# A hand-written order for the opening stage of a Fourier–Hyena and latent-attention block, and another order of its projections

## The chip, the cores and the metric

The kernel runs on one core of one Trainium2 chip. Its time is device microseconds (us) of one launch. A core has five engines with a queue each: TensorE (PE, matmuls and, beside them, weight loads, PEld), VectorE (DVE), ScalarE (ACT), GpSimd (POOL) and SyncE (SP, which here issues the DMAs). They run side by side and wait for each other by semaphores. SBUF is the on-chip memory with 128 partitions; PSUM is the smaller one into which PE accumulates.

## The reference

Two layers over an image sequence x (512 tokens of 1024) and a context (256 tokens of 1024). Layer 0 mixes tokens with a Fourier and a Hyena half, layer 1 with latent attention; each has a convolutional FFN. The change sits in layer 0's mixer. Cut to that:

```python
def _adaln(cond, w_mod, b_mod):
    return jnp.split((jax.nn.silu(cond) @ w_mod + b_mod)[:, None, :], 6, axis=-1)

def _hyena_filter_spectrum(L, w1, b1, w2, b2, w3, b3, w4, freq):
    ...                                        # z: 33 features of each position
    h = jnp.sin(f * (z @ _f32(w1) + _f32(b1)))
    h = jnp.sin(f * (h @ _f32(w2) + _f32(b2)))
    h = jnp.sin(f * (h @ _f32(w3) + _f32(b3)))
    h = h @ _f32(w4)
    h_fwd = h[:, :D_HYENA] * decay
    h_bwd = h[:, D_HYENA:] * decay
    two_sided = jnp.concatenate([h_fwd, zeros(1, D_HYENA), h_bwd[:0:-1]], axis=0)
    two_sided = two_sided / jnp.sum(jnp.abs(two_sided), axis=0, keepdims=True)
    return jnp.fft.rfft(two_sided, axis=0)

def _fourier_hyena_mixer(h, w_in, w_out, conv_w, conv_b, ...):
    proj = h @ w_in                                              # 1024 -> 2048
    y_f = fft2(proj[..., :512], axes=(1, 3)).real                # in 4 groups of 128
    x0, x1, v = jnp.split(_dwconv3(proj[..., 512:], conv_w, conv_b), 3, axis=-1)
    y_h = x0 * _long_conv(v * x1, spectrum, hy_bias)
    return jnp.concatenate([y_f, y_h], axis=-1) @ w_out

# layer 0, with shift, scale and gate of _adaln for x and for the context
hx = _rms_norm(x, norm1) * (1 + sc1) + sh1
x = x + g1 * _fourier_hyena_mixer(hx, ...)
x = x + g2 * _conv_ffn(...)
# the context goes the same way with its own modulation and a filter of its own length
```

## The kernel before

Activations lie transposed: eight tiles of 128 features, x in columns 0 to 511 and the context in 514 to 769 of the same tile (772 columns). To keep float32 accuracy, most operands are split in two, a rounded high part (`hi`, L98, on ACT) and the rest (`lo`, L103, on DVE), and a product is three matmuls (`mm3`: L117 high by high, L118 weights' high by low, L119 weights' low by high). In the tables of the profile a matmul shows as `mm<-hh,wh`: output, then input and weights. Two PSUM pools serve all: `mm` (1024 columns, 3 buffers) and `ms` (512 columns, 2 buffers). Streamed weights come through the pool `W` of three buffers each for the raw tile `wr` and its two halves `wh` and `wl` (`wload`, L105).

**The opening.** What must be there before the first projection: the normed and modulated inputs hh and hl, eight tiles each. What must be there before the spectral stage: the filters' spectra. Its parts:

- `filter_mlp` (L318): three layers, each one matmul (L331) and a sine, which is seven steps on DVE and the Sin on ACT (L306 to L316). It ends in h3, for 6 blocks of 128 positions (4 of x's filter, 2 of the context's).
- `filter_time` (L336), for each block: two 512-column matmuls with w4 (L346), one for the forward and one for the backward half; the products with the decay (L352, L353); in the first block the backward half's first row set to zero (L355); sum and difference of the halves on POOL (L358), each split (`aph`, `apl`, `amh`, `aml`); the absolute values of both halves (ACT, L365 and L366), their sum (POOL, L367), a matmul with a constant tile that sums over positions (L372), and a reciprocal S (L374).
- `filter_spec` (L377): the row of hy_bias, `brow`, is scaled (L382); the Nyquist row (L390 to L393); then for each of 2 or 4 frequency blocks a `wload` of the transform's table, the `mm3` over the filter's blocks, and the scaling by S (L404 to L406).
- `gemv_pe` (L171): one of four chunks of adaLN's shift and scale. Its 2 MB weights come in two DMAs (L177) into a pool `wm` of three, then eight matmuls (L180), a copy (L183), four small matmuls (L186) and the bias add (L191). `make_A` (L209) follows.
- `norm` (L212): `stat` squares a tile (ACT, L224) and sums it on PE (L225); `fin` copies, transposes the sums to columns (L233), runs an inverse square root of twelve tiny DVE steps (L121 to L138) and spreads it with a matmul against the identity (L239), R; `apply` for each of the eight tiles, x and context, scales by A and R (DVE, L249), adds the shift into hh (ACT, L251) and forms hl (DVE, L252).

They are called in this order: network; adaLN chunk 0; the context's filter in time; chunk 1; the context's spectrum; x's filter in time; chunk 2; x's statistics and R; chunk 3; the context's statistics and R; A; two frequency blocks of x's spectrum; sixteen `apply`; the other two. A scheduler of the kernel's framework lays out each engine's queue from that, so the order on an engine is not just the order of the calls.

**The projections.** `proj(m)` (L474), sixteen times: `wload` of a 1024 by 128 part of w_in, 48 matmuls over hh and hl, and a `gemv_dve` (L193), which computes one 128-feature tile of the rest of adaLN on DVE (a DMA into `wr`, L201, L202), so that DVE is used beside PE; 16 of the 32 such tiles `gl` go here, the rest into the `hook` of the w_out projection (two for each call). `hconv(m)` is a projection with its three-tap convolution (ACT L295, DVE L296 and L297). For each of four feature blocks v and x1 are projected, multiplied and folded (`fold`: POOL L490 and L491, DVE L495 and L496), and later transposed on PE (`turn`: six transposes L502) and split into `uTh` and `uTl`, which the spectral stage reads. The order of the calls:

```python
for i in range(4):
    hconv(12 + i, cv)
    if folded:
        turn(i - 1, folded.pop())
    hconv(8 + i, cx)
    folded.append(fold(i, cv, cx))
hconv(4, x0[0])
turn(3, folded.pop())
for i in range(1, 4):
    hconv(4 + i, x0[i])
for g in range(4):
    nc.scalar.copy(Uf[g], proj(g)[:, :TW])
```

**After that.** `spectral` for the context and for x, the inverse transforms, `fourier` for four groups (Uf), the w_out projection, FFN 0 (w_up, L710 on; a `fill` does three `gemv_dve` tiles of layer 1 with each of the first blocks), attention and FFN 1.

## Time and profile before

| | |
|---|---|
| time, median of 3 runs | 1839.36 us (1838.71 to 1841.66) |
| the profiled execution: its own time | 1836.58 us |
| its span (first to last instruction) | 1834.8 us |
| mean granted clock of PE over the span | 0.957 |
| busy in the span: PE, PEld, DVE, ACT, POOL | 93%, 72%, 55%, 33%, 7% |
| chain that ended last: PE, DVE, ACT, POOL | 78%, 11%, 4%, 3% |
| read from HBM, mean rate | 167.23 MB, 93 GB/s |
| opening / projections / rest of the mixer (from, to) | 0 to 135 / 135 to 275 / 275 to 386 us |
| w_out and FFN 0 / attention / o-projection and FFN 1, roughly | 386 to 1000 / 1000 to 1420 / 1420 to 1834 us |

A line of a timeline gives the start, the duration of one instruction, its engine, its line in the kernel (L331 is line 331), its operation, the tiles as output<-inputs, and its shape; a bracket names the idle time of the engine before it and what ended that. PE's granted clock is the share of its full speed that it was allowed in a stretch. PE at 93% means that some 120 us of the span are without a matmul; the table of windows in the prediction shows that 37 of them lie in the opening.

### The profile page before, as it was taken

What the parts mean: (1) busy time and instruction counts of PE and PEld (TensorE: products, weight loads), DVE (VectorE), ACT (ScalarE), POOL (GpSimd) and SP (SyncE); (2) the same over time, 40 slices, a digit from 0 to 9 for tenths busy, and PEclk for the clock granted to TensorE, in tenths of its full rate; (3) what the DMA queues carried; (4) which work ended last, traced back from release to release, by engine and by line L of the source; (5) the groups of instructions that cost most, each with busy time, mean ns of one, the idle gap of its engine ahead of it and who ended that gap; (6) DMA issues with size and microseconds to landing.
All of it is one profiled execution on the core that took longest, in us unless ns stands there. A gap on an engine that the chain in (4) does not pass through costs nothing.

```text
span 1834.8 us, 21694 instructions
## 1 busy us (share of the span) xinstructions
PE 1714.6 (93%) x8742; PEld 1328.5 (72%) x8742; DVE 1015.0 (55%) x1663; ACT 613.2 (33%) x830; POOL 122.7 (7%) x202
## 2 busy tenths in 40 slices
PE   5789996799899999999999887899998999999999
PEld 2358885687688888888888565555554778888887
DVE  4668735887886434543233554666664554444443
ACT  2332212322422212221122334665663443223231
POOL 1401103310000000000000000110110000000000
PEclk8889996799999999999999998899999999999999
DMA  9213320355255223432112320000002323322322
GB/s 355 75 58 127 114 84 20 118 179 166 104 172 170 106 92 134 153 104 69 47 63 78 110 74 24 1 12 12 12 12 69 115 69 99 108 92 92 104 75 98
DMA packets 53249, 172.83 MB, mean 94 GB/s; under 512 B 6043, under 2 KB 8925, under 8 KB 52125
## 3 DMA queue, kind: packets, MB, share of 16 engines
q1 hardware_dynamic: 53149, 171.45, 27.2%
q8 instruction: 69, 1.13, 0.2%
q14 instruction: 31, 0.25, 0.0%
HBM read 167.23 MB, written 4.19 MB: 93 GB/s over the span
## 4 chain that ended last, share of the span: by engine, by line
PE 78%; DVE 11%; ACT 4%; POOL 3%; issue 2%; DMA 1%; SPq 0%; POOLq 0%; ACTq 0%; DVEq 0%
PE mm L117 22%; PE mm L118 21%; PE mm L119 21%; PE pv L1053 2%; PE z L1041 2%; PE ms L225 2%; DVE wl L103 1%; DVE S L1031 1%; DVE junk L201 1%; PE s L1007 1%; DVE hl L252 1%; ACT S L1022 1%; PE s L117 1%; PE s L118 1%; PE s L119 1%
## 5 line engine op out<-in xcount | busy, mean ns | idle before, releaser
L117 PE MATMUL mm<-hh,wh 128*128 128x512 f32 (+2 forms) x1344 | 473.5, 355 | 4.4 <-ACT hh L251 4.1
L118 PE MATMUL mm<-hl,wh 128*128 128x512 f32 (+2 forms) x1344 | 473.2, 353 | 2.6 <-DVE hl L252 2.3
L119 PE MATMUL mm<-hh,wl 128*128 128x512 f32 (+2 forms) x1344 | 472.8, 352 | 1.3 <-DVE wl L103 1.3
L98 ACT ACTIVATE wh<-wr 128x1024 fp32r<-128x1024 f32 (+2 forms) x200 | 206.3, 1032 | 714.2 <-PE mm L118 657.2
L103 DVE TENSOR_TENSOR wl<-wr,wh 128x1024 fp32r<-128x1024 f32 (+2 forms) x200 | 242.3, 1212 | 308.4 <-ACT wh L98 300.7
L117 PEld LDWEIGHTS mm<-hh,wh 128*128 128x128 f32 x1344 | 253.9, 189 | 53.2 <-issue 11.1
L118 PEld LDWEIGHTS mm<-hl,wh 128*128 128x128 f32 x1344 | 254.1, 189 | 41.2 <-DVE hl L252 5.0
L119 PEld LDWEIGHTS mm<-hh,wl 128*128 128x128 f32 x1344 | 253.8, 189 | 38.1 <-issue 2.5
L117 PE MATMUL mm<-ah,wh 128*128 128x512 f32 (+1 forms) x528 | 187.9, 356 | 0.0
L118 PE MATMUL mm<-al,wh 128*128 128x512 f32 (+1 forms) x528 | 187.8, 356 | 0.0
L119 PE MATMUL mm<-ah,wl 128*128 128x512 f32 (+1 forms) x528 | 187.4, 355 | 0.0
L201 DVE SCALAR_TENSOR_TENSOR junk<-wr,sb 128x1024 bf16<-128x1024 f32 x128 | 157.6, 1231 | 30.4 <-DMA wr<-wmodT 30.0
L685 DVE SCALAR_TENSOR_TENSOR xr<-mm,mod,xr 128x512 f32<-128x512 f32 (+1 forms) x100 | 62.1, 641 | 198.9 <-PE mm L119 198.7
L117 PEld LDWEIGHTS mm<-ah,wh 128*128 128x128 f32 x528 | 99.1, 188 | 19.3 <-DVE xr L685 2.5
L118 PEld LDWEIGHTS mm<-al,wh 128*128 128x128 f32 x528 | 99.3, 188 | 15.3 <-issue 0.8
L119 PEld LDWEIGHTS mm<-ah,wl 128*128 128x128 f32 x528 | 99.2, 188 | 14.5
L1022 ACT ACTIVATE S<-s,rks 128x512 f32<-128x512 f32 x96 | 63.3, 688 | 44.0 <-PE s L119 43.1
L1031 DVE TENSOR_TENSOR S<-S,mb 128x1536 f32<-128x1536 f32 x32 | 54.8, 1751 | 20.7 <-POOL mb L1028 20.7
L722 ACT ACTIVATE fg<-fg 128x772 f32<-128x772 f32 (+1 forms) x44 | 32.6, 740 | 100.3 <-DVE fg L297 89.7
L1053 PE MATMUL pv<-S,V 128*64 128x512 f32 x192 | 58.9, 621 | 0.0
L1041 PE MATMUL z<-S,ones 128*32 128x512 f32 x192 | 42.7, 699 | 13.8 <-ACT S L1032 11.3
L1032 ACT ACTIVATE S<-S 128x1536 f32<-128x1536 f32 x32 | 47.1, 1482 | 18.3 <-DVE S L1031 18.3
(317 smaller groups left out, 2300.6 us busy)
## 6 DMA issues: line engine op xcount, KB each, us to landing
wr<-w_up SPq DMA_DIRECT2D x88, 512.0 KB, 3.2
wr<-wmodT SPq DMA_DIRECT2D x80, 512.0 KB, 3.3
wr<-w_dn SPq DMA_DIRECT2D x32, 512.0 KB, 3.3
wm<-wmod0a SPq DMA_DIRECT2D x8, 1024.0 KB, 8.6
wr<-w_in SPq DMA_DIRECT2D x16, 512.0 KB, 3.3
wr<-w_dn SPq DMA_DIRECT2D x20, 384.0 KB, 3.0
wr<-w_out SPq DMA_DIRECT2D x12, 512.0 KB, 4.2
wr<-w_o SPq DMA_DIRECT2D x12, 512.0 KB, 3.2
```

Of the source, the lines that this page charges most:

```text
L98: self.nc.scalar.activation(dst, src, AF.Copy)
L103: (eng or self.nc.vector).tensor_tensor(dst, src, hi.bitcast(F32), op=ALU.subtract)
L117: mmul(out, wh, xh, start=start, stop=False)
L118: mmul(out, wh, xl, start=False, stop=False)
L119: mmul(out, wl, xh, start=False, stop=stop)
L201: nc.vector.scalar_tensor_tensor(junk, raw, 1.0, self.sb[:, j, :], op0=ALU.mult, op1=ALU.mult, accum_out=acc)
L685: nc.vector.scalar_tensor_tensor(x[m][:, a2:b2], ps[:, a2:b2], mod[:, 8 * sec + m, j : j + 1], x[m][:, a2:b2], op0=ALU.mult, op1=ALU.add)
L1022: nc.scalar.activation(S[j // 3][:, j % 3, :], ps, AF.Copy, scale=rs[:, 2 * j + a : 2 * j + a + 1])
L1031: v.tensor_tensor(s, s, mb3.to_broadcast([P, 3, T]), op=ALU.subtract)
L1032: nc.scalar.activation(s, s, AF.Exp)
L1041: nc.tensor.matmul(z[32 * g : 32 * g + 32, :], self.ones32, Ss[g // 2][(2 * k + g % 2) // 3][:, (2 * k + g % 2) % 3, :], start=k == 0, sto ...
L1053: nc.tensor.matmul(pv[64 * a : 64 * a + 64, :], V[:, k, 64 * h : 64 * h + 64], Ss[a][k // 3][:, k % 3, :], start=k == 0, stop=k == 5, tile ...
```

## The change

It rewrites the opening and reorders the projections; what is computed is the same. In its parts:

- **An order by hand.** The opening stands in a `manual_schedule` block for all five queues, so each engine takes its instructions in the order of the calls. New order, in short: network's layers 0 and 1; x's statistics; layer 2; x's R; the context's filter blocks 4 and 5 on PE; chunk 0; the decay products; block 0; the context's statistics; splits; block 1; absolute values; the context's R; chunk 1; the context's spectra with its norm sum between; blocks 2 and 3; Nyquist row; chunk 2; splits; x's first spectrum; x's norm sum; chunk 3; A; then the `apply` steps, split into `scaled` (L249, L251) and `low` (L252) and interleaved with the three other spectra and their splits, and the first two w_in tiles. The DMAs of x, the context, the decays, `brow`, the first three chunks of adaLN's weights and the first three transform tables are issued at the head (`gemv_raw`, which is the DMA part of `gemv_pe`, and `wraw`, that of `wload`).
- **Sum and difference in the weights.** POOL forms w4's sum and difference once (`w4pm`), so the matmul gives sum and difference of the halves at once, each multiplied by the decay. Row 0 of a filter's first block, whose backward half is zero, is overwritten by two one-row matmuls with w4's forward half. The norm then uses |p + m| + |p − m|, with p the sum and m the difference, and half the constant: POOL forms p + m and p − m, ACT both absolute values, and all of them go into the norm's sum as matmuls (four for the context in place of two, eight for x in place of four). The low part of the difference (`aml`) is formed by POOL, that of the sum by DVE.
- **The projections' order.** Uf[0] and Uf[1] first, the four x0 convolutions, then the four pairs with their turns, then `turn(3)`, then Uf[2] and Uf[3]. In the changed kernel's code the six transposes of a turn are L624, the norm sum's matmuls are in `filter_sum`, and so on.
- **Later loads.** `load_sb` and with it the `gemv_dve` tiles are held back (`issue_after`) behind the last steps that form h, until Uf[1] is projected.
- **Eight adaLN tiles move.** The `hook` of the w_out projection leaves eight of the tiles, and FFN 0's `fill` does them first.

The diff, cut to its core:

```diff
-        def apply(d):
+        def scaled(d):
             A, B = self.A[i][k][:, j, :], self.mod[i][:, 24 * k : 24 * k + 8, j]
-            u = tp()
+            u = box[d] = tp()
             nc.vector.scalar_tensor_tensor(u[:, :n], x[d][:, c0 : c0 + n], A[:, d : d + 1], box["R"][:, :n], op0=ALU.mult, op1=ALU.mult)
-            dst = hh[d][:, c0 : c0 + n]
-            nc.scalar.activation(dst, u[:, :n], AF.Identity, bias=B[:, d : d + 1])
-            nc.vector.scalar_tensor_tensor(hl[d][:, c0 : c0 + n], u[:, :n], B[:, d : d + 1], dst.bitcast(F32), op0=ALU.add, op1=ALU.subtract)
+            return nc.scalar.activation(hh[d][:, c0 : c0 + n], u[:, :n], AF.Identity, bias=B[:, d : d + 1])
+        def low(d):
+            B = self.mod[i][:, 24 * k : 24 * k + 8, j]
+            return nc.vector.scalar_tensor_tensor(hl[d][:, c0 : c0 + n], box.pop(d)[:, :n], B[:, d : d + 1], hh[d][:, c0 : c0 + n].bitcast(F32),
+                                                  op0=ALU.add, op1=ALU.subtract)
+        def apply(d, step=None):
+            if step != 1:
+                ins = scaled(d)
+            if step != 0:
+                ins = low(d)
+            return ins
...
+        self.w4pm = self.t(p, [P, 1024], F32, "w4pm")
+        w4 = [self.t(self.S2, [P, 512], F32, "s2") for _ in range(2)]
+        self.w4 = w4[0]
         nc.sync.dma_start(zT, I["zT"])
         nc.sync.dma_start(fw, I["fw"])
-        nc.sync.dma_start(w4, I["w4"])
-        h = zT
-        for l in range(3):
+        for q in range(2):
+            nc.sync.dma_start(w4[q], I["w4"][:, 512 * q : 512 * q + 512])
+        for q, op in ((0, ALU.add), (1, ALU.subtract)):
+            nc.gpsimd.tensor_tensor(self.w4pm[:, 512 * q : 512 * q + 512], w4[0], w4[1], op=op)
...
+    def filter_mm(self, h3, tt, first=False):
+        ps = self.mm()
+        r0, c = 64 * (tt // 3), 128 * (tt % 3)
+        for q in range(2):
+            s = slice(512 * q, 512 * q + 512)
+            self.nc.tensor.matmul(ps[:, s], h3[r0 : r0 + 64, c : c + 128], self.w4pm[r0 : r0 + 64, s], start=True, stop=True)
+        if first:
             for q in range(2):
+                self.nc.tensor.matmul(ps[0:1, 512 * q : 512 * q + 512], h3[r0 : r0 + 64, c : c + 1], self.w4[r0 : r0 + 64, :], start=True, stop=True)
+        return ps
+    def filter_pm(self, ps, dec):
+        parts = []
+        for q, tg in enumerate(("ap", "am")):
+            s = self.t(self.S2, [P, 512], F32, "s2")
+            self.nc.vector.tensor_tensor(s, ps[:, 512 * q : 512 * q + 512], dec, op=ALU.mult)
+            hi = self.t(self.pf, [P, 512], F32R, tg + "h", 4)
+            self.hi(hi, s)
+            parts.append((s, hi))
+        return parts
+    def filter_lo(self, parts):
+        out = []
+        for tg, (s, hi), eng in zip(("ap", "am"), parts, (None, self.nc.gpsimd)):
+            lo = self.t(self.pf, [P, 512], F32R, tg + "l", 4)
+            self.lo(lo, s, hi, eng)
+            out.append((hi, lo))
+        return out
+    def filter_abs(self, parts):
+        (p_, _), (m_, _) = parts
+        f = self.t(self.S2, [P, 512], F32, "s2")
+        self.nc.gpsimd.tensor_tensor(f, p_, m_, op=ALU.add)
+        self.nc.gpsimd.tensor_tensor(m_, p_, m_, op=ALU.subtract)
+        self.nc.scalar.activation(f, f, AF.Abs)
+        self.nc.scalar.activation(m_, m_, AF.Abs)
+        return [f, m_]
+    def filter_sum(self, sums, nhalf):
         ps = self.ms()
         on = self.onesN[nhalf]
         for i, f in enumerate(sums):
+            self.nc.tensor.matmul(ps, on, f, start=i == 0, stop=i == len(sums) - 1)
         S = self.t(self.pf, [P, 512], F32, "S")
+        self.nc.vector.reciprocal(S, ps)
+        return S
...
-            v.memset(self.onesN[nh], nh)
+            v.memset(self.onesN[nh], 0.5 * nh)
...
+        ENG = mybir.EngineType
+        with self.tc.manual_schedule(engines={ENG.PE, ENG.DVE, ENG.SP, ENG.Activation, ENG.Pool}):
+            layer = self.filter_mlp()
+            for d in range(KD):
+                nc.sync.dma_start(x[d][:, 0:512], I["xT"][d])
+            dec = {}
+            def decays(*tts):
+                for tt in tts:
+                    dec[tt] = tp()
+                    nc.sync.dma_start(dec[tt], I["decay"][tt])
+            decays(4, 5)
+            wm = [self.gemv_raw(0)]
+            decays(0, 1)
+            for d in range(KD):
+                nc.sync.dma_start(x[d][:, C0 : C0 + C], I["cxT"][d])
+            wm.append(self.gemv_raw(1))
+            decays(2, 3)
+            nc.sync.dma_start(self.brow, I["hyb"].partition_broadcast(P))
+            tc_ = [self.wraw(I["ftab"][ft, :, 0:512], 512) for ft in range(2)]
+            wm.append(self.gemv_raw(2))
+            tx = [self.wraw(I["ftab"][0])]
+            h = layer(1, layer(0, None))
+            for d in range(KD):
+                s1(d)
+            h3 = layer(2, h)
+            f1(True)
+            pc = [self.filter_mm(h3, 4, True), self.filter_mm(h3, 5)]
+            self.gemv_pe(0, 0, wm[0])
+            wm.append(self.gemv_raw(3))
+            pmc = [self.filter_pm(pc[i], dec[4 + i]) for i in range(2)]
+            px = [self.filter_mm(h3, 0, True)]
+            for d in range(KD):
+                s2(d)
+            ac = [self.filter_lo(pm) for pm in pmc]
+            pmx = [self.filter_pm(px[0], dec[0])]
+            px.append(self.filter_mm(h3, 1))
+            fc = [f for pm in pmc for f in self.filter_abs(pm)]
+            pmx.append(self.filter_pm(px[1], dec[1]))
+            f2(True)
+            self.gemv_pe(0, 1, wm[1])
+            ax = [self.filter_lo(pm) for pm in pmx]
+            self.filter_skip(256.0)
+            twc = [self.wsplit(r, 512) for r in tc_]
+            Hc = []
+            pcs = []
+            for ft in range(2):
+                pcs.append(self.filter_spec(ac, twc[ft]))
+                if ft == 0:
+                    Sc = self.filter_sum(fc, 256.0)
+                    px.append(self.filter_mm(h3, 2))
+                    pmx.append(self.filter_pm(px[2], dec[2]))
+                Hc.append(self.filter_scale(pcs[ft], Sc))
+            fx = [f for pm in pmx[:2] for f in self.filter_abs(pm)]
+            px.append(self.filter_mm(h3, 3))
+            pmx.append(self.filter_pm(px[3], dec[3]))
+            nyc = self.filter_nyquist(ac, Sc)
+            self.gemv_pe(0, 2, wm[2])
+            ax += [self.filter_lo(pm) for pm in pmx[2:]]
+            twx = [self.wsplit(tx[0])]
+            fx += [f for pm in pmx[2:] for f in self.filter_abs(pm)]
+            psx = self.filter_spec(ax, twx[0])
+            S = self.filter_sum(fx, 512.0)
+            self.filter_skip(512.0)
+            self.gemv_pe(0, 3, wm[3])
+            self.make_A(0, 0)
+            self.close("wm")
+            hp = self.pool("hp", side="right")
+            for d in range(KD):
+                hh.append(self.t(hp, [P, TW], F32R, f"hh{d}"))
+                hl.append(self.t(hp, [P, TW], F32R, f"hl{d}"))
+            self.zero_pads(hh + hl)
+            def both(d, step):
+                a1(d, step)
+                return a2(d, step)
+            twx.append(self.wload(I["ftab"][1]))
+            both(0, 0)
+            H = [self.filter_scale(psx, S)]
+            both(1, 0)
+            both(0, 1)
+            psx = self.filter_spec(ax, twx[1])
+            twx.append(self.wload(I["ftab"][2]))
+            both(2, 0)
+            both(1, 1)
+            ny = self.filter_nyquist(ax, S)
+            both(3, 0)
+            both(2, 1)
+            H.append(self.filter_scale(psx, S))
+            psx = self.filter_spec(ax, twx[2])
+            twx.append(self.wload(I["ftab"][3]))
+            both(4, 0)
+            both(3, 1)
+            both(5, 0)
+            both(4, 1)
+            win = [self.wload(I["w_in"][0])]
+            both(6, 0)
+            both(5, 1)
+            last_act = both(7, 0)
+            both(6, 1)
+            last = both(7, 1)
+            H.append(self.filter_scale(psx, S))
+            win.append(self.wload(I["w_in"][1]))
+            H.append(self.filter_scale(self.filter_spec(ax, twx[3]), S))
...
+        behind = ExitStack()
+        behind.enter_context(self.tc.issue_after(last.ins))
+        behind.enter_context(self.tc.issue_after(last_act.ins))
         self.load_sb()
...
+        for g in range(2):
+            nc.scalar.copy(Uf[g], proj(g)[:, :TW])
+        behind.close()
+        for i in range(4):
+            hconv(4 + i, x0[i])
...
-        hconv(4, x0[0])
         turn(3, folded.pop())
-        for i in range(1, 4):
-            hconv(4 + i, x0[i])
-        for g in range(4):
+        for g in range(2, 4):
...
-                if gl:
+                if len(gl) > 8:
...
-        gl1 = [(1, jt, (0, 1) if jt < 16 else (0,)) for jt in range(48)]
+        gl1 = gl + [(1, jt, (0, 1) if jt < 16 else (0,)) for jt in range(48)]
```

More of the change, by code (lines that the diff above doesn't have):

```diff
@@ L381, in filter_spec @@
         B = self.brow
[L382 removed]
+        self.nc.vector.tensor_scalar(B, B, self.bscale / nhalf, None, op0=ALU.mult)
         self.bscale = nhalf
[L384 to L393 removed]
@@ L408, in filter_spec, with filter_nyquist @@
-        return H, ny
+    def filter_nyquist(self, a, S):
+        v = self.nc.vector
+        ps = self.ms()
+        nt = len(a)
+        for i in range(nt):
+            for q in range(2):
+                self.nc.tensor.matmul(ps[0:1, :], self.altr, a[i][0][q], start=i == 0 and q == 0, stop=i == nt - 1 and q == 1)
+        ny = self.t(self.S2, [P, 512], F32, "s2")
+        v.tensor_tensor(ny[0:1, :], ps[0:1, :], S[0:1, :], op=ALU.mult)
+        v.tensor_tensor(ny[0:1, :], ny[0:1, :], self.brow[0:1, :], op=ALU.add)
+        return ny
@@ new lines, in filter_spec, with filter_scale @@
+    def filter_spec(self, a, tb):
+        nt = len(a)
+        th, tl = tb
+        ps = self.mm()
+        for c in range(2):
+            for i in range(nt):
+                w = slice(256 * i + 128 * c, 256 * i + 128 * c + 128)
+                self.mm3(ps[:, 512 * c : 512 * c + 512], th[:, w], tl[:, w], a[i][c][0], a[i][c][1], i == 0, i == nt - 1)
+        return ps
+    def filter_scale(self, ps, S):
+        v = self.nc.vector
+        hr = self.t(self.S2, [P, 512], F32, "s2")
+        hi = self.t(self.S2, [P, 512], F32, "s2")
+        v.tensor_tensor(hr, ps[:, 0:512], S, op=ALU.mult)
+        self.nc.gpsimd.tensor_tensor(hr, hr, self.brow, op=ALU.add)
+        v.tensor_tensor(hi, ps[:, 512:1024], S, op=ALU.mult)
+        return hr, hi
@@ L474, in proj @@
         def proj(m):
-            wh, wl = self.wload(I["w_in"][m])
+            wh, wl = win[m] if m < 2 else self.wload(I["w_in"][m])
             ps = self.mm()
```

119 lines of the change are left out of this document (18 added, 101 removed).

## The prediction

> **What bounds the kernel now.** The page first: PE is busy 93% of the span and carries 78% of the chain that ended last, so time can come only from stretches in which PE is not fed. The table of windows by stage shows where they are (stretch, its length, busy us of PE, PE's weight load, DVE, ACT, POOL, granted PE clock, DMA share, GB/s):
> ```profile
> 0.00:135.00 135.00, 97.85 (x351) 49.40 (x351) 77.90 (x146) 43.38 (x75) 34.27 (x58) 0.85 0.45 166
> 135.00:275.00 140.00, 137.25 (x766) 118.01 (x767) 94.40 (x154) 34.75 (x40) 15.19 (x24) 0.99 0.31 107
> 275.00:386.00 111.00, 81.67 (x445) 72.18 (x443) 83.10 (x143) 38.92 (x69) 37.20 (x60) 0.77 0.22 76
> ```
> The opening has 37 us without PE work, the projections 3. The change rewrites the first and reorders the second. The third (spectra and Fourier mixing) waits on DVE and POOL, and its order is the same in both built programs: it only shifts.
>
> Next, the timelines of PE and of DVE over the opening (start, duration, line, tiles, and in brackets the idle time before and what ended it):
> ```profile
> 107.72 0.48 PE L118 MATMUL mm<-aml,wh 128*128 128x512 f32 x1
> 108.04 0.40 PE L119 MATMUL mm<-amh,wl 128*128 128x512 f32 x1
> 113.49 1.20 PE L239 MATMUL ms<-cst,rq_r 128*128 128x128 f32 x4 [5.05 <-DVE rq_r L135]
> ...
> 120.67 0.79 PE L117 MATMUL mm<-aph,wh 128*128 128x512 f32 x1 [2.57 <-DVE s L406]
> 121.26 0.63 PE L118 MATMUL mm<-apl,wh 128*128 128x512 f32 x1
> ```
> ```profile
> 9.58 0.43 DVE L382 TENSOR_SCALAR brow<-brow 128x512 f32<-128x512 f32 x1 [1.97 <-DMA brow<-hyb]
> ...
> 29.37 0.69 DVE L352 TENSOR_TENSOR s<-mm,s 128x512 f32<-128x512 f32 x1 [1.74 <-PE mm L346]
> ...
> 33.67 1.09 DVE L103 TENSOR_TENSOR apl<-s,aph 128x512 fp32r<-128x512 f32 x1 [1.82 <-ACT aph L98]
> 34.90 0.69 DVE L103 TENSOR_TENSOR aml<-s,amh 128x512 fp32r<-128x512 f32 x1 [0.15 <-ACT amh L98]
> ```
> The norm's statistics come last, so the sixteen `apply` steps start only at 121.7, and the first projection, from 129.0, starves on hh and hl. Behind the idle 5.05 us PE steps its 512-column matmuls every 0.43 us until 126.4; before and later it does so every 0.23.
>
> Last, the chain from a pair's last convolution to its transposes (ACT, DVE and POOL timelines; the projection's matmuls end at 170.1), and the transposes on PE:
> ```profile
> 171.02 0.98 ACT L295 ACTIVATE tm<-mm,pcol 128x772 f32<-128x772 f32 x1
> ```
> ```profile
> 172.29 1.02 DVE L296 SCALAR_TENSOR_TENSOR tm<-mm,pcol,tm 128x771 f32<-128x771 f32 x1
> 173.22 1.22 DVE L201 SCALAR_TENSOR_TENSOR junk<-wr,sb 128x1024 bf16<-128x1024 f32 x1
> ...
> 174.36 1.02 DVE L297 SCALAR_TENSOR_TENSOR tm<-mm,pcol,tm 128x771 f32<-128x771 f32 x1
> ...
> 177.76 0.94 DVE L495 TENSOR_TENSOR tm<-tm 128x256 f32<-128x256 f32 x1 [1.18 <-POOL tm L490]
> ```
> ```profile
> 175.52 2.21 POOL L490 TENSOR_TENSOR tm<-tm,tm 128x512 f32<-128x512 f32 x1 [15.30 <-DVE tm L297]
> ```
> ```profile
> 178.85 0.98 PE L502 MATMUL mm<-cst,tm 128*128 128x128 f32 x6 [0.31 <-DVE tm L495]
> ```
> It takes 8.7 us, and PE waits for 0.31 of them, since the next projection's 48 matmuls stand between.
>
> **The yardstick.** Without a turn in it a projection takes 8.45 us (the splits L103 of its weights start at 250.99, 259.44 and 267.89). Two projections and a turn take 18.16 (transposes at 178.85 and 197.01), so a turn costs 1.26. The first spectral matmul starts at 275.2; back from there, 16 × 8.45 + 4 × 1.26 = 140.2 gives a clean start of the projections at P = 135.0. I sum the new P, and then the new end of the projections.
>
> **The opening.** I walk the built queues in the order in which they stand, with durations from rows of before.
> - Sine network. The wait for brow goes: 2.3 us gained (the first Sin from 12.87 to 10.6; a layer is 5.93, from 12.87 to 18.81). But PE now has the eight statistics matmuls ahead of layer 2's: eight squares (84.20, 4.26 us) sit on ACT in between. h3 at 27.7, against 25.3.
> - All of the norm's closing step for x stands ahead of the filters on PE: copy 0.6, row sums 1.0, twelve tiny DVE steps 2.4, broadcast 1.2 to 2.1 at the lower clock. PE reaches the filters at 33.2. Block 4: two matmuls and two one-row ones, each 1.05 at full speed or 1.8 at the lower clock (27.35: six half-matmuls, 5.39); I take 5.5, since PE was idle before. Block 5 2.2, adaLN chunk 0 2.2, its copy and tail 1.6. DVE's queue has that chunk's bias add ahead of the decays, so these start at 44.8, where before has 29.4. What is bought: x's R is ready at 34, not at 98.5.
> - Four decay products 2.4. Then POOL: two lows and four sums and differences, 6 × 1.3, to 54.7. ACT's abs wait for these, and the context's statistics copy stands behind the abs: its closing step (0.5 + 2.4 + 0.9) ends at 60.6, chunk 1 with its tail at 64.6, two lows, brow and a 512 split (2.3) at 66.9; I add 1 for DVE and POOL in each other's way: 67.9.
> - The context's spectrum 2.6, its norm sum 4 × 1.04 (twice the matmuls of before), reciprocal 3.4, decay 1.2, scale 1.2, to 80.3 (block 3 needs the PSUM tile that the scale frees); block 3 2.1, Nyquist 0.95, chunk 2 and tail 3.5, two lows and a 1024 split 2.4: 89.3.
> - x's first spectrum 22 × 0.233 = 5.1, sum 8 × 1.04 = 8.3, reciprocal 3.4 (chunk 3's tail waits for it, for a PSUM tile), tail 1.0, bias and A 0.5, split 1.15: 108.8. The sixteen `apply` steps can start, 13 us sooner than before.
> - DVE to the split of the first projection: six scales and five lows at 1.06 a block, three 1024 splits 3.45, two spectra scaled 2.4, Nyquist 1.3, small gaps 1.2: 20.0. PE's three remaining spectra (3 × 5.6) end about then. With 1.2 for POOL: P = 130. Gain 5.
>
> Both ends: everything on PE at full speed and POOL never in DVE's way takes 3.1 off up to 44.8 and 4 behind: P = 123. POOL at 2.2 instead of 1.3 (as at 175.52, beside a DVE step) and chunk 1 and the spectra slow: P = 137. I take 130, since the rows show both clocks.
>
> At this place the Trainium skill, SBUF — State Buffer, section Who interferes with whom, speaks against the change: a DVE step with two SBUF inputs and a GpSimd step that reads SBUF shut each other out for the whole instruction. The trace agrees (the first low, beside POOL, took 1.09 us, the second 0.69), and the change puts six of the lows on POOL; by that rule P lies nearer to 137.
>
> **The last turn.** Before, `turn(3)` stands behind `hconv(4)`, whose projection covers the chain. In the changed PE queue the six transposes L624 stand directly behind the 48 matmuls of `hconv(11)`, whose fold they read, and the projections of Uf[2] and Uf[3] behind them. Nothing covers the chain: to the ACT start 0.9, then 1.27 (ACT and a split), 0.93 (no gemv step is queued here), 1.16, POOL 1.3 with DVE idle (as at 157.24) or 2.2, a fold 1.1: 6.7 us idle, 7.6 at most. Then PE is slow: behind the idle 5.5 us at 61.8 two half-matmuls L372 took 2.08, not 1.04, and chunk 2 3.18, not 1.85: 2.4 lost. So turn 3 costs 6.7 + 1.0 + 2.4 = 10.1.
>
> The Trainium skill, TensorE: Matmul & The Clock Gate, Part 1, says the clock halves after an idle window of about 3.4 us and returns after as much work. The slow matmuls behind both idle stretches agree; by it an estimate of the loss is 1.7, and the sum 0.7 us lower.
>
> **What is hidden.** Eight gemv tiles move into the first FFN: 16 × 1.3 = 21 us of DVE. Both stretches are PE's: 25.00 busy of 25 from 400 to 425 and from 425 to 450, and 50.00 of 50 in each window from 500 to 950, where DVE is at 44 of 50 falling to 20. So nothing; up to 21 if DVE were last there, and at best 4.9 less, the five PE gaps from 463 to 483 — but DVE's order there is unchanged. The third projection's weights can be fetched only when DVE reaches the opening's last splits (137): DMA 3.3, split on ACT and DVE and three gemv steps 6, at 146, against 147 when PE asks: 0, at worst 3. All the opening's loads land by about 50, at the 400 GB/s of windows 10 to 40.
>
> **Sum.** 130 + 16 × 8.45 + 3 × 1.26 + 10.1 = 279.1 for the first spectral matmul, against 275.2: +3.9. The profiled execution took 1836.6 (span 1834.8, 1.8 around it), so 1840.5; the runs' median is 1839.4, 2.8 above it, so 1843 there. A difference below 0.2%, 3.7 us, can't be told from none.
>
> **Rivals.**
> - Faster: PE keeps its full clock, in the opening and behind turn 3. P = 123, no 2.4: 269.7, −5.5, 1834. For: 0.23 us steps from 72 to 107 across short gaps. Against: the slow stretches at 30 to 42 and 54 to 72 with as sparse a queue. It decides if the first scaled step starts before 103.
> - Much slower: POOL blocks DVE throughout and the opening gains nothing, P = 137: +10.9, 1850. For: the 1.09 and 2.21 rows, and the sum and difference are not saved but moved, from the matmul's output into the abs (POOL has 26 large steps in place of 24). Against: half of the lows beside POOL are off the path.
> - That turn 3 does not stall: −4.9, 1834; only if another PE step stood between, and the built queue has none. Counted with the first.
>
> **Numbers.** My forecast 0.50, the first rival 0.25, the second 0.25. The forecast's own range, P from 126 to 134, is 0 to +8 us, half of it inside 0.2%. So faster 0.25, same 0.25, slower 0.50; one sign does not hold most of it, and the range takes in both rivals, 1834 to 1851.
>
> **What would show it.** Right: decays at about 45, the first scaled step at about 109, the first hh matmul at 130 without gaps in its projection, an idle 6.7 us before L624's last group with 0.43 us steps behind it, the first spectral matmul at 279. Wrong: a scaled step before 103, no idle time before that turn, or new PE gaps from 500 on.

## The result: 20 us slower, outside the range

The changed kernel took 1859.08 us (median of 4 runs, 1857.76 to 1860.65), the kernel before beside it 1839.62 (4 runs): a ratio of 1.0105, 95% interval 1.0087 to 1.0122. The forecast was 1843, the range 1834 to 1851. The profiled execution took 1860.65 with a span of 1858.9, which is 24.1 above that of before; the medians differ by 19.5, because before's profiled execution lies 3 below its median and this one 1.6 above.

The table of windows by stage of the changed kernel (same stretches and columns as before):

```profile
0.00:135.00 135.00, 91.56 (x278) 42.67 (x279) 51.72 (x95) 33.01 (x61) 33.01 (x59) 0.74 0.38 139
135.00:275.00 140.00, 138.24 (x755) 117.68 (x754) 112.47 (x187) 41.22 (x49) 14.62 (x9) 0.99 0.40 128
275.00:386.00 111.00, 75.80 (x400) 64.97 (x399) 69.64 (x111) 32.99 (x54) 34.43 (x56) 0.82 0.18 59
```

In the first 135 us PE runs 278 instructions, not 351, at a granted clock of 0.74, not 0.85, and DVE is busy for 52 us, not 78: the opening is not done. The checkpoints (us from the span's start):

| | before | forecast | changed |
|---|---|---|---|
| first decay product | 29.4 | 44.8 | 53.3 |
| first scaled step (L249, now L258) | 121.7 | 108.8 | 130.5 |
| first projection matmul | 129.0 | 130 | 152.5 |
| idle ahead of the last turn | 0.3 | 6.7 | 6.73 |
| first spectral matmul | 275.2 | 279.1 | 302.2 |
| first w_out step (xr, L685, now L809) | 391.5 | | 415.9 |
| end of the span | 1834.8 | | 1858.9 |

All of the loss is there by the spectral stage (27.0); the mixer gives 2.6 back, and from w_out to the end both kernels run in step. PE's timeline shows two places where the opening lost time (as in the prediction: start, duration, line, tiles, and the idle time before):

```profile
34.78 2.05 PE L248 MATMUL ms<-cst,rq_r 128*128 128x128 f32 x8 [2.53 <-DVE rq_r L141]
36.76 3.78 PE L369 MATMUL mm<-w4pm,s 64*128 64x512 f32 x4
40.47 3.57 PE L372 MATMUL mm<-s,s 64*1 64x512 f32 x4
43.97 3.78 PE L369 MATMUL mm<-w4pm,s 64*128 64x512 f32 x4
47.68 3.64 PE L189 MATMUL ms<-wm,sT 128*32 128x512 f32 x16
52.08 1.05 PE L195 MATMUL ms<-cst,s 128*128 128x2 f32 x8 [0.76 <-ACT s L192]
...
96.06 1.92 PE L189 MATMUL ms<-wm,sT 128*32 128x512 f32 x16
103.78 1.87 PE L195 MATMUL ms<-cst,s 128*128 128x2 f32 x8 [5.79 <-ACT s L192]
...
110.37 0.79 PE L125 MATMUL mm<-aph,wl 128*128 128x512 f32 x1 [3.67 <-DVE wl L103]
```

First, from 34.8 to 51.3 PE has work without a break, at a granted clock of 0.50, and its steps take about twice their time: the same adaLN chunk (L189) is 3.64 there and 1.92 at 96.06, a filter block (L369) 3.78 there and 1.98 at 88.23. Second, at 98.0 PE stops for 5.79 on ACT's copy of chunk 2 (L192) and then for 3.67 on a split. ACT's timeline has the reason:

```profile
97.34 0.63 ACT L400 ACTIVATE s<-s 128x512 f32<-128x512 f32 x1 [0.72 <-POOL s L398]
99.02 0.63 ACT L401 ACTIVATE s<-s 128x512 f32<-128x512 f32 x1 [1.04 <-POOL s L399]
100.24 0.63 ACT L400 ACTIVATE s<-s 128x512 f32<-128x512 f32 x1 [0.59 <-POOL s L398]
101.58 0.63 ACT L401 ACTIVATE s<-s 128x512 f32<-128x512 f32 x1 [0.71 <-POOL s L399]
...
103.16 0.56 ACT L192 COPY s<-ms 128x512 f32<-128x512 f32 x1
```

The copy could run at 98.0. It stands behind four absolute values, and each of those waits for one of POOL's sums and differences.

### The profile page after: what moved, and what is told of

The parts are those of the page before. It is cut to its first block, busy times and chain, and to the rows that moved or that the text cites. A ratio compares the mean times of both kernels' runs of the same rounds, so it can differ in the third digit from the quotient of the medians.

```text
span 1858.9 us, 21743 instructions
## 1 busy us (share of the span) xinstructions
PE 1724.4 (93%) x8762; PEld 1334.1 (72%) x8762; DVE 1015.6 (55%) x1654; ACT 613.8 (33%) x830; POOL 123.5 (7%) x204
## 4 chain that ended last, share of the span: by engine, by line
PE 69%; DVE 7%; ACT 3%; POOL 2%; issue 1%; POOLq 0%; ACTq 0%; DVEq 0%
PE mm L123 19%; PE mm L125 19%; PE mm L124 19%; PE pv L1177 2%; PE z L1165 2%; PE ms L234 1%; DVE S L1155 1%; PE s L1131 1%; ACT S L1146 1%; PE s L123 1%; PE s L124 1%; PE s L125 1%; DVE wl L103 1%; POOL mb L1152 1%; DVE nt L258 1%
## 5 line engine op out<-in xcount | busy, mean ns | idle before, releaser
L809 DVE SCALAR_TENSOR_TENSOR xr<-mm,mod,xr 128x512 f32<-128x512 f32 (+1 forms) x100 | 62.2, 642 | 202.9 <-PE mm L125 202.6
L1165 PE MATMUL z<-S,ones 128*32 128x512 f32 x192 | 42.7, 699 | 13.7 <-ACT S L1156 11.3
```

What stands on the lines that cost most here:

```text
L809: nc.vector.scalar_tensor_tensor(x[m][:, a2:b2], ps[:, a2:b2], mod[:, 8 * sec + m, j : j + 1], x[m][:, a2:b2], op0=ALU.mult, op1=ALU.add)
L1165: nc.tensor.matmul(z[32 * g : 32 * g + 32, :], self.ones32, Ss[g // 2][(2 * k + g % 2) // 3][:, (2 * k + g % 2) % 3, :], start=k == 0, sto ...
```

## The experiments

The theories after the result: **clock** (the new sequence leaves PE's queue so thin that it runs at half speed), **queue heads** (in an order by hand an instruction that waits holds up what stands behind it), **formula** (the matmuls and POOL steps that sum and difference in the weights add), **POOL** (its steps hold DVE up), **projections' order** (the uncovered turn). Ratios are to the kernel before, run on the same chip, with 95% intervals. Its own median was between 1837.4 and 1839.6 beside the different runs, so a difference of two medians in the text carries some 2 us; the ratios don't.

| run | median us | ratio | first scaled step | first spectral matmul |
|---|---|---|---|---|
| e1_turn | 1852.53 | 1.0077 (1.0062 to 1.0092) | 129.1 | 290.7 |
| e2_sched | 1865.40 | 1.0155 (1.0138 to 1.0172) | 135.0 | 302.8 |
| e3_weights | 1836.60 | 0.9993 (0.9984 to 1.0003) | 120.9 | 273.4 |
| e4_oldfilter | 1859.52 | 1.0115 (1.0100 to 1.0130) | 127.7 | 298.5 |
| e5_projorder | 1851.01 | 1.0071 (1.0049 to 1.0094) | 123.6 | 286.4 |
| e6_chunk2 | 1852.78 | 1.0090 (1.0067 to 1.0114) | 123.3 | 293.7 |
| e7_amldve | 1859.12 | 1.0122 (1.0099 to 1.0144) | 130.3 | 300.9 |
| e8_warm | 1852.89 | 1.0083 (1.0064 to 1.0102) | 119.4 | 290.4 |
| e9_both | 1849.14 | 1.0060 (1.0039 to 1.0082) | 114.2 | 284.6 |
| e10_beforeproj | 1856.40 | 1.0106 (1.0082 to 1.0129) | 129.4 | 297.3 |
| e11_three | 1838.10 | 1.0002 (0.9993 to 1.0011) | 115.4 | 277.1 |
| e12_projcovered | 1835.13 | 0.9988 (0.9977 to 0.9998) | 124.3 | 276.8 |
| e13_best | 1832.16 | 0.9968 (0.9956 to 0.9980) | 121.3 | 272.8 |

**The clock: fillers in PE's idle places.**

```diff
+    def warm(self, n):
+        for _ in range(n):
+            self.nc.tensor.matmul(self.dummy[:, 0:128], self.ident, self.ident, start=True, stop=True)
...
+            h = layer(0, None)
+            self.warm(16)
+            h = layer(1, h)
+            self.warm(12)
...
-            f1(True)
+            f1(True, (14, 7))
...
-            f2(True)
+            f2(True, (7, 7))
```

The pairs stand ahead of the row sums and of the broadcast of R.

> The changed kernel with idle places of PE's queue up to 71 us filled with matmuls of a constant by itself, whose result nothing reads (16 and 12 in the network, 14 and 7 in x's closing step, 7 and 7 in the context's). Clock theory (the granted clock was 0.59 from 40 to 80, and PE was busy 19.2 of 20 us from 40 to 60): with a full clock the PE-bound stretch from 34.8 to 51.3 falls from 16.5 to some 9, the decays come at 46 instead of 53, the context's spectrum at 70 instead of 79, the first scaled step at 121 to 124, the time 1850 to 1853. Queue-head theory: the filters come earlier, but ACT and POOL end as late: the first scaled step at 127 or later and the time at most 3 us less; if the fillers themselves run late, slower.

The first scaled step came at 119.4, 11.1 earlier and more than expected; the time fell by 6.2, by the ratios by 4, and there the two intervals overlap. What is clear of noise is the gain in the opening. The stretch from 40 to 80, first in the changed kernel, then with the fillers (columns as above):

```profile
40.00:80.00 40.00, 31.41 (x96) 9.96 (x96) 13.05 (x29) 12.54 (x26) 10.49 (x8) 0.59 0.18 67
```
```profile
40.00:80.00 40.00, 35.81 (x142) 17.77 (x143) 15.45 (x30) 12.54 (x26) 10.48 (x8) 0.79 0.26 96
```

The granted clock rises from 0.59 to 0.79; doing more, PE is done sooner. In the profiled execution the gain was 11.3 at w_out and 8.2 at the end. It was lost in attention, whose code and order are untouched: from the last convolution step of FFN 0 (`fg` on ACT) to the first of FFN 1 it took 500.6, against 497.0 in the changed kernel. The two other runs with fillers have the same 500.4 and 500.6, and a run without them (e4_oldfilter) 499.9; what decides it was not found, so a difference of 3 us at the end between single executions is no finding here.

**The queue head: chunk 2 ahead of four absolute values.**

```diff
-            fx = [f for pm in pmx[:2] for f in self.filter_abs(pm)]
             px.append(self.filter_mm(h3, 3))
             pmx.append(self.filter_pm(px[3], dec[3]))
             nyc = self.filter_nyquist(ac, Sc)
             self.gemv_pe(0, 2, wm[2])
+            fx = [f for pm in pmx[:2] for f in self.filter_abs(pm)]
```

> The changed kernel with one call moved: adaLN chunk 2 stands ahead of the absolute values of x's blocks 0 and 1, so its copy on ACT no longer waits behind POOL. Queue-head theory: the 5.8 us that PE idles ahead of chunk 2's tail and most of the 3.7 behind it are gained, and PE keeps its clock: the first scaled step at 124 or earlier instead of 130.5, the time 1852 or less. Clock theory or POOL theory: POOL's eight sums and differences (about 12 us in a row from 96 to 111) then end as late as before and the norm sum waits for them: the first scaled step within 2 us of 130.5, the time within 2 of 1859.

The first scaled step came at 123.3, 7.2 earlier, of which 1.1 was there before the edit's place (the decays at 52.2): 6.1 for the queue head. The time, 1852.8, is just above the 1852 expected. PE's timeline:

```profile
94.65 1.92 PE L189 MATMUL ms<-wm,sT 128*32 128x512 f32 x16
97.33 1.05 PE L195 MATMUL ms<-cst,s 128*128 128x2 f32 x8 [0.76 <-ACT s L192]
102.13 0.79 PE L123 MATMUL mm<-aph,wh 128*128 128x512 f32 x1 [3.75 <-ACT wh L98]
...
104.52 0.79 PE L125 MATMUL mm<-aph,wl 128*128 128x512 f32 x1 [1.17 <-DVE wl L103]
```

The tail waits for 0.76, not 5.79. The next instruction that stands behind the absolute values on ACT, the split of the table, now costs 3.75.

**Both.** The two edits together, nothing else.

> The changed kernel with both edits that moved the first scaled step: the fillers in PE's idle places up to 71 us, and adaLN chunk 2 ahead of the absolute values of x's blocks 0 and 1. If clock and queue head are two separate losses they add up: the first scaled step 11.1 and 6 to 7 us earlier than 130.5, at 112 to 114, close to the 109 that was forecast, the first spectral matmul at 283 to 285 instead of 302.2, the time 1846 to 1848. If they are one loss seen twice (a late chunk 2 only because PE was slow): at 118 or later, the time 1851 or more.

114.2 and 284.6: they nearly add up, two separate losses, 16.3 us together of the 17.2 that 11.1 and 6.1 make. The time, 1849.1, was 10 below the changed kernel's (8 by the ratios, whose intervals no longer overlap) and 1 above the expected range; the mixer took 104.8 us instead of 102.2 (below), and attention 500.4. Even so the opening wins nothing: the first scaled step is 7.5 earlier than in the kernel before, but the first projection matmul comes at 135.0, against 129.0, since the new order puts the three remaining spectra of x between the two.

**The formula, from both sides.** In the kernel before, sum and difference in the weights alone (the scheduler's order):

```diff
+        for q, op in ((0, ALU.add), (1, ALU.subtract)):
+            nc.gpsimd.tensor_tensor(self.w4pm[:, 512 * q : 512 * q + 512], w4[0], w4[1], op=op)
...
-            v.tensor_tensor(f, ps[:, 0:512], dec, op=ALU.mult)
-            v.tensor_tensor(b, ps[:, 512:1024], dec, op=ALU.mult)
+                v.tensor_tensor(s, ps[:, 512 * q : 512 * q + 512], dec, op=ALU.mult)
...
+            sums += [f, pm[1]]
```

> The kernel before with one part of the change alone: sum and difference formed in the weights, the one-row matmuls, the norm over sum and difference with twice the matmuls, the low part of the difference on POOL; the order is the scheduler's. Formula theory: the added matmuls (two pairs of one-row ones at 3.6 a pair, six more in the norm sums at 0.5 to 0.6) and POOL steps lie on the path: 8 us or more slower, 1847 to 1853, the clean start of the projections from 135 to 143 or later. Hand-order theory: within 3 us of 1839, since the scheduler fits them in where PE idles (37 of the opening's 135 us).

And the changed kernel's order with the old formula (w4 itself, sum and difference on POOL, `fc` and `fx` with one tile for each block):

> The changed kernel with its hand-written order, but the filters computed as before: matmuls with w4 itself, sum and difference of the halves on POOL, no one-row matmuls, half as many matmuls in the norm sums, all low parts on DVE. Formula theory: from the changed kernel's rows, 3.6 for the one-row matmuls ahead of chunk 0, 2.2 and 3.3 for the norm sums and 1.9 for the first sine that POOL's work on the weights blocks, less 2.6 for POOL's step ahead of the splits: 8.4 us less, the first scaled step at 122, the time 1851. Hand-order theory: POOL's step is now ahead of every split and the queue on PE is no denser: at most 4 us less, 1855 or above.

Neither shows a cost: 0.9993 with 1 inside the interval, and 1859.5 against 1859.1. In the second the scaled step is 2.8 earlier (8 were expected of the formula), and its profiled execution, 3.7 ahead at w_out, lost 3.0 of that again in attention. So the formula is not the loss; a part of some 3 us of it in the changed kernel's opening is not excluded.

**POOL.** One argument: the low part of the difference on DVE.

```diff
-        for tg, (s, hi), eng in zip(("ap", "am"), parts, (None, self.nc.gpsimd)):
+        for tg, (s, hi), eng in zip(("ap", "am"), parts, (None, None)):
```

> The changed kernel with the low parts of the difference on DVE instead of POOL. POOL theory (a POOL step on SBUF beside a DVE step with two SBUF inputs holds it up: two lows took 3.13 us at 55.65 beside POOL's 2.95, against 1.28 at 77.14 alone): DVE does four lows in 2.6 where it took 3.1, and POOL's queue, on the path twice, is shorter by 2.6 each time: 3 to 5 us less, the first scaled step at 126 to 128. Rival: DVE's queue is longer by 1.2 in each of the two places and nothing else moves: within 2 us of 1859.

No change, 1859.1. DVE's four lows took 0.68 each, where two beside POOL had taken 3.13, so a low beside POOL does take longer; but behind them DVE waited for PE's one-row matmuls (L372, 1.02 idle) and the decay product stayed at 58.3, as against 58.7.

**The order by hand.** The same calls, laid out by the scheduler.

```diff
-        with self.tc.manual_schedule(engines={ENG.PE, ENG.DVE, ENG.SP, ENG.Activation, ENG.Pool}):
+        with ExitStack():
```

> The changed kernel with the same calls in the same sequence, but without the hand-written order: the scheduler lays out the five queues of the opening. Hand-order theory (instructions that wait stand at the heads of in-order queues: ACT's copy for adaLN chunk 2 behind absolute values that wait for POOL, PE's filters behind x's norm): the first scaled step comes well before 130.5, at 122 or earlier, and the time falls by 8 us or more, to 1851 or below. Formula theory (the added matmuls and POOL steps are the loss, in whatever order): the first scaled step stays at 128 or later and the time within 4 us of 1859.

Slower, 1865.4: neither theory had that. The scheduler put the scaling of `brow`, which starts only when its load has landed, at 33.6 in this sequence, and two splits ahead of layer 1's sine on DVE's queue, which idled 21.2 us there; the second Sin ran at 39.8 instead of 18.4. The order by hand is not worse than the scheduler's of this sequence; both have a queue head of their own.

**The projections' order, from both sides.**

```diff
-        turn(3, folded.pop())
         for g in range(2, 4):
             nc.scalar.copy(Uf[g], proj(g)[:, :TW])
+            if g == 2:
+                turn(3, folded.pop())
```

In the changed kernel:

> The changed kernel with the last turn moved behind the projection of Uf[2], so that 48 matmuls cover its chain. Projection-order theory: the 9.4 us that this turn costs in the changed kernel (6.73 idle, slow transposes and matmuls behind it) fall to the 1.26 of a covered turn: the first spectral matmul at 294.0 instead of 302.2, the time about 1851 (8 us less). Rival, that the rest of the mixer gives such microseconds back anyway (between the first spectral matmul, 27.0 us late, and the first w_out step, 24.4 us late, 2.6 were regained): no more than 5 us less, 1854 or above.

In the kernel before, the changed order as it is, and the same with the last turn covered:

> The kernel before with the changed kernel's order of the projections alone (Uf[0], Uf[1], the x0 convolutions, the four pairs, the last turn uncovered, Uf[2], Uf[3]). Projection-order theory: the uncovered turn costs 8.2 more than a covered one, as in the changed kernel: the first spectral matmul at 283.4 instead of 275.2, the time 1847. Rival, that the scheduler pulls the next projection ahead of the transposes or that the mixer regains the loss: within 3 us of 1839.

> The kernel before with the changed order of the projections, but with the last turn covered by the projection of Uf[2]. If the 13.5 us of that order are the uncovered turn (8.2 in the trace) and slower work in the mixer behind it, both go or only the first: 1838 to 1843. If Uf first and the x0 convolutions early cost something of their own (the opening's end starves the projections longer, or the mixer runs at a lower clock): 1844 or above.

Covering the turn gained 6.5 in the changed kernel (5 by the ratios) and 15.9 (1851.0 to 1835.1) in the kernel before, where the uncovered turn had been expected to cost 8. With cover the order costs nothing. In the changed kernel the first spectral matmul came 11.5 sooner, 2.5 of them from ahead of the projections and 9.0 from the turn, and the mixer gave 2.6 back, as the rival had it in part. PE's timeline, uncovered in the changed kernel, then covered (e1_turn):

```profile
282.56 1.51 PE L624 MATMUL mm<-cst,tm 128*128 128x128 f32 x6 [6.73 <-DVE tm L617]
```
```profile
281.61 0.82 PE L624 MATMUL mm<-cst,tm 128*128 128x128 f32 x6
```

In the kernel before, the first spectral matmul is 9.6 later without cover. The rest of the 15.9 goes with a lower clock further on. From the first spectral matmul to w_out, and w_out up to its first step, with the turn uncovered and covered (e5_projorder, e12_projcovered):

```profile
286.40:392.30 105.90, 78.56 (x423) 70.48 (x421) 77.12 (x130) 37.23 (x65) 33.80 (x46) 0.76 0.20 63
392.30:406.60 14.30, 11.98 (x51) 9.88 (x50) 7.91 (x19) 1.84 (x5) 5.05 (x46) 0.76 0.95 327
```
```profile
276.80:379.00 102.20, 71.48 (x423) 63.36 (x422) 77.07 (x130) 36.88 (x65) 33.76 (x46) 0.82 0.21 65
379.00:390.50 11.50, 9.15 (x51) 7.52 (x50) 7.90 (x19) 1.85 (x5) 5.05 (x46) 1.00 0.97 333
```

The same instructions, a clock of 0.76 against 0.82 and of 0.76 against 1.00: 3.7 and 2.8 us. In the profiled executions the mixer's code took between 99.9 and 105.9 without being changed; what decides in which places the clock falls was not found.

**The old order behind the new opening.**

> The changed kernel's opening with the projections in the order of the kernel before (the first two w_in tiles that the opening splits are those of that order's first two projections). With the run of the other order alone (13.5 slower than before, 8.2 of it the uncovered turn by its trace) two readings stand: if the order costs only the turn, this gains 6.5 to 8, as covering the turn did, 1851 to 1853; if the order costs 13 whatever the opening, it gains 12 to 14 and the opening itself is worth 6 to 8, 1845 to 1847.

1856.4, 2.7 less than the changed kernel's and by the ratio no less (1.0106 and 1.0105), and neither reading. The first spectral matmul came only 4.9 sooner: the distances between turns were 18.4, 20.5 and 19.6 instead of 18.2, with PE idle for 2.61 ahead of the third. DVE's row ahead of that turn, then PE's:

```profile
208.56 1.23 DVE L210 SCALAR_TENSOR_TENSOR junk<-wr,sb 128x1024 bf16<-128x1024 f32 x1 [1.89 <-DMA wr<-wmodT]
```
```profile
217.53 1.51 PE L624 MATMUL mm<-cst,tm 128*128 128x128 f32 x6 [2.61 <-DVE tm L617]
```

A `gemv_dve` step waits 1.89 for its weights, and the split and the convolution, whose ACT parts are done by 208.3, stand behind it: another queue head. Whether it explains all of it was not tried.

**What is left, and a better kernel.** On top of all that had helped, w4's two loads and POOL's sum and difference of them (`weights`) go behind x's loads:

```diff
             for d in range(KD):
                 nc.sync.dma_start(x[d][:, 0:512], I["xT"][d])
+            self.weights()
```

> The changed kernel with the fillers, chunk 2 moved and the last turn covered, and one more edit: w4's two loads and POOL's sum and difference of them stand behind the loads of x, so that POOL no longer works beside the first sine (its three DVE steps took 3.62 us there, 1.74 in the other layers). If that is part of the 5.4 us still open between the forecast 108.8 and the 114.2 reached so far: the first Sin at 10.6 instead of 12.5, the first scaled step at 112 to 112.5, the time 1840 to 1842 (1849.1 less 6.5 for the turn and 1.9). Rival: the load comes too late for the filters or POOL then blocks another DVE step, the first scaled step stays at 114 or later, the time 1843 or above.

The time reached that of the kernel before: 1838.1, below the 1840 to 1842 expected. But the new edit gained nothing, as the rival had it for the scaled step (115.4), though not for the time: covering the turn made the first spectral matmul 7.5 earlier than in e9_both, and the mixer took 99.9 instead of 104.8, the shortest of all runs, so part of the time is luck or unexplained. DVE's timeline, the three sine steps in the changed kernel (layers 0 and 1), then in this one (layer 1):

```profile
8.41 3.62 DVE L333 SCALAR_TENSOR_TENSOR s<-s,s 128x384 f32<-128x384 f32 x3
...
16.23 1.74 DVE L333 SCALAR_TENSOR_TENSOR s<-s,s 128x384 f32<-128x384 f32 x3
```
```profile
13.74 3.63 DVE L335 SCALAR_TENSOR_TENSOR s<-s,s 128x384 f32<-128x384 f32 x3
```

POOL's work now fell beside layer 1's sine instead of layer 0's. Last, the kernel before with the two parts that cost nothing alone:

> The kernel before, its opening laid out by the scheduler as it was, with the two parts of the change that cost nothing by themselves: sum and difference formed in the weights (0.9993 alone) and the projections' order with the last turn covered (0.9988 alone). If the two small gains are real and separate: a ratio of about 0.998, 1833 to 1835, both kernels beaten. If they are scatter of the clock in the mixer's sparse stretch: a ratio within 0.1% of 1.

1832.2, 0.9968 (0.9956 to 0.9980): a little faster than both kernels, and than the 0.9981 that the two parts make together, within the intervals. It has nothing of the order by hand.

## Why the prediction was wrong

The forecast's walk against the trace, each stretch's own length:

| stretch of the opening | forecast | measured |
|---|---|---|
| to h3 and PE's filters | 33.2 | 36.8 |
| filters 4 and 5, chunk 0, to the decays | 11.6 | 16.5 |
| to the context's spectrum, full flow | 23.1 | 26.1 |
| context's spectrum to x's (blocks 2 and 3, chunk 2) | 21.4 | 31.0 |
| x's spectrum, norm sum, to the first scaled step | 19.5 | 20.1 |
| to the projections' clean start P | 21.2 | 23.3 |
| 16 projections, 3 turns | 139.0 | 139.0, taken over |
| turn 3 | 10.1 | 9.4 |

(The 139.0 is the forecast's yardstick, not a measurement; the distances between the first three turns, 18.16 and 18.15, agree with it. P is 302.2 less 139.0 less the turn's 9.4, 153.8; the turn is the time from the end of the matmuls ahead of it to the end of the last projection, 26.3, less 16.9 for two projections.) The first five rows give 21.7 of the 23.1 by which the first spectral matmul missed the forecast.

- **"Block 4 … I take 5.5, since PE was idle before. Block 5 2.2, adaLN chunk 0 2.2": mis-sized, shown.** They took 7.2, 3.7 and 3.6. The step let the slow clock end after some matmuls; it lasted for 16.5 us of unbroken work and came back in later stretches. With fillers 11.1 us of the opening were gained. Of the 3.6 of the table's first row, 1.9 is another term, put at nothing: the first Sin ran at 12.5, not 10.6, behind three DVE steps that took 3.62 beside POOL's work on w4.
- **"Chunk 2 and tail 3.5": the step that failed, shown.** It was walked on PE alone. ACT's copy stands behind four absolute values that wait for POOL, and the table's split behind more; in the forecast that queue was followed for the context ("the context's statistics copy stands behind the abs") and not here. From the chunk's start to x's spectrum the forecast had 5.9 (3.5, and 2.4 for lows and a split); it took 14.3, and 9.9 with the chunk moved. The move gained 6.1 at the first scaled step. With both edits PE still idles 3.75 and 1.16 at that place, and the 9.9 is 4 more than forecast, most of the 5.4 that separate 114.2 from 108.8. That this last piece is the split's place on ACT is read from the rows, not tried.
- **Both ends of P, 123 to 137: too narrow.** The upper end added POOL's blocking and some slow matmuls, and no time for a head of a queue.
- **The rival "POOL blocks DVE throughout": right side, wrong cause.** DVE's steps do take longer beside POOL (3.62 against 1.74, 3.13 against 1.28 for two lows). The Trainium skill, SBUF — State Buffer, section Who interferes with whom, says that such steps contend. Taking the lows off POOL changed nothing, so the time did not hang on them; POOL's sums and differences stayed in that run, and through ACT's absolute values they are part of the queue head.
- **The last turn: right.** Idle 6.73 (6.7 forecast), slow matmuls behind it, 9.4 against 10.1. Less 6.7 and 1.0 for the transposes, the slow clock cost 1.7, not the 2.4 of the rows. The estimate that the prediction had worked out from the Trainium skill, TensorE: Matmul & The Clock Gate, Part 1, was 1.7. That the mixer behind an uncovered turn can also run at another clock was not foreseen; in the kernel before that took a further 6.5 us, in the changed one it gave 2.6 back. That the turn causes it is not shown.
- **"The third only shifts": wrong by its clock.** With an unchanged order the mixer up to the first w_out step ran 2.6 us shorter than before, within the scatter of the runs.
- **What is hidden: right.** From w_out's first step to the end the kernel before takes 1443.3 us with PE busy for 1393.05, the changed kernel 1443.0 with 1392.70, with the eight adaLN tiles moved. The later loads were not tried alone; no loss shows in the distances of the turns.

The faster rival wanted PE at full clock; the fillers made that true for much of the opening, and the first scaled step was still at 119.4, later than the 103 from which it decides.

## What to carry to other kernels

Walk each queue of a hand-written order to the end, not just the bounding engine's: for every wait on any engine write down what stands behind it, above all short copies that the bounding engine waits for. Before pricing a sparse stretch of matmuls at their full-speed duration, ask what has kept PE dense just before; if nothing has, price it at the slow duration too, and let the range take in both. Let one block of independent matmuls stand between a result and its transposes.

## What the runs showed of the hardware

Unbroken work did not soon bring PE's clock back. In the changed kernel 16.5 us without a gap (34.8 to 51.3) stayed at half speed, and but for the first 2 us all of it was matmuls with weights of 64 rows, of one column or of 32 columns; at 52.08, behind 0.76 of idle time, the clock was full (1.05, against 1.87 at 103.78), and at 55.04 it was half again (L372, 3.57). Without the one-column matmuls it was no different: in e4_oldfilter two filter blocks took 7.19 from 34.28 on and chunk 0 behind them 3.43. The Trainium skill, TensorE: Matmul & The Clock Gate, Part 1, lets the clock return after some 3.4 us of sustained work; here the measurement says otherwise. Behind 14 and 7 fillers of 128 by 128, the same matmuls soon ran at full speed (e9_both):

```profile
35.80 2.54 PE L376 MATMUL mm<-w4pm,s 64*128 64x512 f32 x4
38.27 1.87 PE L379 MATMUL mm<-s,s 64*1 64x512 f32 x4
40.07 1.98 PE L376 MATMUL mm<-w4pm,s 64*128 64x512 f32 x4
41.98 1.92 PE L189 MATMUL ms<-wm,sT 128*32 128x512 f32 x16
...
47.87 3.57 PE L379 MATMUL mm<-s,s 64*1 64x512 f32 x4
```

They were slow again at 47.87, with no idle time above 0.76 us between. With matmuls of 128 by 128 by 512 the clock was back after 5.7 us (110.4 to 116.1 in the changed kernel). That small matmuls count for less is the likely reading; no run varied their size alone.
